# A hybrid encoder block in one kernel: the first receptance projection is taken from the unscaled input

## The chip, the cores and the metric

The kernel runs as one program on one core of a Trainium2 chip. The metric is the device time of one execution in microseconds (us); less is better. The engines of the core are named as the profile names them: PE is TensorE (PEld its weight load), DVE is VectorE, ACT is ScalarE, POOL is GpSimd, SP is SyncE, which issues most DMAs.

## The reference

One layer with 512 tokens of width 1024: an RMS norm, one wide input projection, three mixers (a gated convolution, an RG-LRU, and RWKV-7 time mixing), a gated merge, an output projection, and a squared-ReLU MLP. Cut to what the change touches:

```python
h = rms_norm(x, norm1_g[l])                 # x * rsqrt(mean(x^2) + eps) * g
p = h @ w_in[l]
pa, pb, pg, pc = _split(p, (COLS_A, COLS_B, COLS_GATE, COLS_C))
...
pc = token_shift(pc, rwkv_mu[l])            # p + (prev - p) * mu
r, k, v, xw, xa, xg = _split(pc, (D_C, D_C, D_C, R_W, R_A, R_G))
w_log = -jax.nn.softplus(-(rwkv_w0[l] + jnp.tanh(xw) @ rwkv_w2[l])) - 0.5
decay = jnp.exp(-jnp.exp(w_log))
a = jax.nn.sigmoid(rwkv_a0[l] + xa @ rwkv_a2[l])
g_c = jax.nn.sigmoid(xg) @ rwkv_g2[l]
kk = k * rwkv_kk[l]                         # then normalised by head
k = k * (1.0 + (a - 1.0) * rwkv_ka[l])
...
yc = rwkv7_recurrence(r, decay, k, v, kk, a)
```

The factor of the norm belongs to a token, and the projection sums over channels. So a projection may be taken from `x * g`, and its result multiplied by the factor of each token afterwards.

## The kernel before

**Layout.** All activations lie transposed: channels on the 128 partitions, the 512 tokens in the free dimension, so that a 128 x 512 tile is one eighth of the width and fills one PSUM tile. Every matmul of full precision is made of three (`mm3`, lines 152 to 155): each operand is split into a high and a low part, and high x high, high x low and low x high are summed. A projection of 128 output columns is thus 8 k tiles x 3 = 24 matmuls of 128 x 512 into one PSUM tile.

**Weights.** `load_w` (lines 123 to 137) fetches a weight tile in two halves. Each half is one DMA of SP into `raw` (3 buffers), a cast on ACT to `whi` (4 buffers) and a subtraction on DVE to `wlo` (4 buffers). These three get a higher priority, so that they stand in the queues well ahead of the matmuls that read them.

**PSUM.** Projections write to the pool `pp` of 3 tiles. Small products use `pm` (2 tiles), the recurrence `pc`.

**The prologue** (lines 204 to 336). `xT` is loaded. For each k tile ACT and DVE make `xgh` and `xgl`, the split of `x * g` without the token factor, and POOL, ACT, DVE and PE sum the squares into `pst`; `rsqrt_rows` turns these into `rsb`, the token factor on all partitions. Meanwhile PE projects from `xgh`, `xgl`: first `t_lr0` and `t_lr1`, the low-rank inputs (xw, xa and xg), and then `t_k0`, the first 128 columns of k (`proj_raw`, lines 258 to 260). Each of these PSUM tiles is multiplied by `rsb` as it is read, by DVE, into an SBUF tile `us0` or `us1` (`unscaled`, lines 296 to 299), from which `shift` (lines 282 to 284: one ACT and one DVE instruction) makes the token shift. `pro_scale` (lines 248 to 256) scales `xT` by `rsb` (five k tiles on POOL, three on DVE) and splits it into `hh` and `hl`, from which all later projections are taken (`proj`, lines 268 to 276).

**After the prologue.** Heads are worked on in four groups. `krv(g)` (lines 372 to 446) prepares k, r, v, decay and gates of a group: the norm of kk (`pn`), the decay (`pw`, then a scan), the gate (`pa`), and from them the tiles `AR` and `BK`. `amat` forms the products `pA` of these, masks them into `AXt` and transposes them to `Z`; `inverse` solves a triangular system on DVE in 31 dependent steps (`dg`, `Z`); `chain` runs the recurrence, `post` norms its result. `ab(q)` computes the two other mixers for 128 channels; it has eight projections (xb, gb, gatb, c, x, b, ga and, elsewhere, gc) and much elementwise work.

**What sets the order.** These parts are generators. `weave` runs a critical one (`krv(0)` first) step by step at a higher priority and, for each of its steps, a number of steps of a filling one (`AB[0]`, with the ratio `R0` = 0.852). A projection has four steps. Each instruction has a priority from where it was written and from the offsets; a scheduler then sets the order of every engine ahead of time, by its own estimate of when operands and buffers are ready. On the chip each engine takes its instructions strictly in this order, and waits in place for semaphores. A name with another number in an order (`pp_271`, `pp_430`) is another tile of the pool, not another buffer.

Of the kernel before, what the change touches and what calls it, by code (L numbers as in the profile page):

```python
# [9 lines left out]
F32 = mybir.dt.float32  # L10
# [8 lines left out]
P = 128  # L19
# [10 lines left out]
S = 512  # L30
# [54 lines left out]
COLS, CN = chunk_plan()  # L85
# [3 lines left out]
def block_kernel(ctx, tc, xt, win, par, mulr, sw, wout, w1, w2, fg, cst, eyes, out):  # L89
# [30 lines left out]
    pv = lambda n, j: part[:, PI[n], j:j + 1]  # L120


    def load_w(src):
        with tc.high_priority(offset=OFF):
            return load_w_(src)
# [10 lines left out]
    def load_w_(src):  # L136
        return [load_half(src, i) for i in range(2)]

    def wslice(w, kt):
        hi, lo = w[kt // 4]  # L140
        sl = slice((kt % 4) * P, (kt % 4 + 1) * P)
        return hi[:, sl], lo[:, sl]
# [49 lines left out]
    pp = ps.enter_context(tc.tile_pool(name="pp", bufs=3, space=PSUM))  # L192
# [65 lines left out]
    def proj_raw(w, t):  # L258
        for kt in range(KT):
            mm3(t, *wslice(w, kt), xgh(kt), xgl[:, kt], start=kt == 0, stop=kt == KT - 1)  # L260
# [7 lines left out]
    def proj(name):  # L268
        w = load_w(win[CN[name]])
        t = pp.tile([P, S], F32, tag="pp", name="pp")  # L270
        for kt in range(KT):
            wh, wl = wslice(w, kt)
            mm3(t, wh, wl, hh[:, kt], hl[:, kt], start=kt == 0, stop=kt == KT - 1)
            if kt % 2 == 1 and kt < KT - 1:
                yield
        return t
# [5 lines left out]
    def shift(pt, mu, omu, o):  # L282
        ac.activation(o, pt, AF.Copy, scale=omu)
        stt(o[:, 1:], pt[:, 0:S - 1], mu, o[:, 1:], MUL, ADD)
# [7 lines left out]
    def WP(tag, bufs=1):  # L292
        return pk.tile([P, S], F32, tag=tag, name=tag, bufs=bufs)


    def unscaled(t, tag):
        o = pro.tile([P, S], F32, tag=tag, name=tag)
        tt(o, t, rsb, MUL)
        return o
# [13 lines left out]
    OMK, OMR, OKA, OMV, N4, P4 = range(6)  # L313
    dvp = lambda i, j: dv[:, i, j:j + 1]
# [2 lines left out]
    shift(unscaled(t_lr0, "us0"), mul[:, 0:1], omul[:, 0:1], lr)  # L317
    t_k0 = pp.tile([P, S], F32, tag="pp", name="pp")
    proj_raw(load_w(win[CN[("k", 0)]]), t_k0)
    ac.activation(lr[0:64], lr[0:64], AF.Tanh)  # L320
    lws = sp.tile([P, S], F32R, name="lws")
    las = sp.tile([P, S], F32R, name="las")
# [10 lines left out]
    lgh, lgl = split(sp, lg, "lg")  # L333
    k0 = WP("ks")
    shift(unscaled(t_k0, "us0"), pv("mu_k", 0), dvp(OMK, 0), k0)
    pro_ctx.close()


# [27 lines left out]
    def c3(t):  # L366
        return t.rearrange("p (c t) -> p c t", c=NC)
# [4 lines left out]
    def krv(g, G_):  # L372
        G_.AR = pk.tile([P, 2, NC, 2, L], F32, tag="AR", name="AR")
        G_.BK = pk.tile([P, 2, NC, 2, L], F32, tag="BK", name="BK")
        G_.pl = sp.tile([P, 2, NC], F32, tag="pl", name="pl", bufs=2)
        G_.v = [sp.tile([P, S], F32, tag=f"v{h}", name=f"v{h}", bufs=2) for h in range(2)]
        G_.bv = [sp.tile([P, S], F32, tag=f"bv{h}", name=f"bv{h}", bufs=2) for h in range(2)]
        for jj in range(2):
            j = 2 * g + jj
            rs = WP("rs")  # L380
            if j == 0:
                ks = k0
            else:
                ks = WP("ks")
                t = yield from proj(("k", j))
                shift(t, pv("mu_k", j), dvp(OMK, j), ks)
            sq = WP("a1")
            ac.activation(sq, ks, AF.Square, scale=pv("kk", j))
            sqh, sql = split(pk, sq, "b")
            pn = pm.tile([P, S], F32, tag="pm", name="pn")  # L390
            pe.matmul(pn, bd, sqh, start=True, stop=False)
            pe.matmul(pn, bd, sql, start=False, stop=True)
            kk = WP("a5")
            rsqrt_rows(pk, kk, pn, 1e-24)
            stt(kk, ks, pv("kk", j), kk, MUL, MUL)
            yield
            t = yield from proj(("r", j))
            shift(t, pv("mu_r", j), dvp(OMR, j), rs)
            yield
            swh, swl = load_sw(pk, "swa", j, 0, 2)  # L400
            pw = pm.tile([P, S], F32, tag="pm", name="pw")
            pe.matmul(pw, swh[:, 0], lws, start=True, stop=False)
            pe.matmul(pw, swl[:, 0], lws, start=False, stop=True)
            sig = WP("a1")
            ac.activation(sig, pw, AF.Tanh, bias=pv("w0", j), scale=0.5)
            v.tensor_scalar(out=sig, in0=sig, scalar1=1.0, scalar2=None, op0=ADD)
            pa = pm.tile([P, S], F32, tag="pm", name="pa")
            pe.matmul(pa, swh[:, 1], las, start=True, stop=False)
            pe.matmul(pa, swl[:, 1], las, start=False, stop=True)
            av = WP("a4")  # L410
            ac.activation(av, pa, AF.Tanh, bias=pv("a0", j), scale=0.5)
            cum = WP("a2")
            v.tensor_tensor_scan(out=cum, data0=smk, data1=sig, initial=0.0, op0=MUL, op1=ADD)
            PP = pk.tile([P, NC, L + 1], F32, tag="PPt", name="PPt")
            gp.memset(PP[:, :, 0:1], 1.0)
            Pt = PP[:, :, 1:L + 1]
            ac.activation(Pt, c3(cum), AF.Exp, scale=-0.5 * CW)
            v.tensor_copy(G_.pl[:, jj], PP[:, :, L])
            pinv = WP("a3")
            ac.activation(pinv, cum, AF.Exp, scale=0.5 * CW)  # L420
            stt(G_.AR[:, jj, :, 0], c3(kk), -1.0, PP[:, :, 0:L], MUL, MUL)
            tt(G_.AR[:, jj, :, 1], c3(rs), Pt, MUL)
            t_ = WP("a1")
            stt(t_, av, 1.0, kk, ADD, MUL)
            stt(G_.BK[:, jj, :, 0], c3(t_), 0.5, c3(pinv), MUL, MUL)
            kp = WP("a2")
            ts2(kp, av, pv("ka", j), dvp(OKA, j), MUL, ADD)
            tt(kp, kp, ks, MUL)
            tt(G_.BK[:, jj, :, 1], c3(kp), c3(pinv), MUL)

            if jj == 0:
                rk = [WP(f"rk{h}") for h in range(2)]
            for h in range(2):
                r = slice(64 * h, 64 * h + 64)
                stt(rk[h][64 * jj:64 * jj + 64], rs[r], part[r, PI["rk"], j:j + 1], kp[r], MUL, MUL)
        rk = [split(pk, rk[h], ("a1", "a3") if h else "b") for h in range(2)]
        for h in range(2):
            q = 2 * g + h
            t = yield from proj(("v", q))
            shift(t, pv("mu_v", q), dvp(OMV, q), G_.v[h])  # L440
            yield
        for h in range(2):
            pb = pm.tile([P, S], F32, tag="pm", name="pb")
            for i in range(2):
                pe.matmul(pb, bd, rk[h][i], start=i == 0, stop=i == 1)
            tt(G_.bv[h], pb, G_.v[h], MUL)
# [450 lines left out]
    with tc.tile_pool(name="mw", bufs=2) as mw, \  # L897
# [12 lines left out]
        for fi in range(NF):  # L910
            t = pp.tile([P, S], F32, tag="pp", name="p1")
# [8 lines left out]
            r = mw.tile([P, S], F32, tag="r", name="r")  # L920
# [141 lines left out]
```

## Time and profile before

| | us |
|---|---|
| time, median of 3 runs | 1146.29 |
| lowest and highest of them | 1145.93 and 1151.92 |
| the profiled execution | 1150.27 |
| its span, from the first to the last record | 1148.5 |
| PE busy in the span | 1114.5 (97%) |
| DVE busy in the span | 787.4 (69%) |
| ACT busy in the span | 548.7 (48%) |
| mean granted clock of PE | 0.988 of full speed |

All times in the rows further down are in us from the start of the span. Busy times of PE are modelled from the starts of pipelined matmuls; a 128 x 512 matmul is shown with some 0.4 us, and the next one starts 0.23 us after it at full clock. A DVE row of 128 x 512 is shown with about 0.69 us, and the next starts 0.60 us after it, since the end of one overlaps the start of the next.

### The profile page before, as it was taken

How to read it: one execution, taken by the hardware profiler on the slowest of the kernel's cores; microseconds unless marked ns; L12 is line 12 of the kernel's file. 1: busy time of each engine (PE TensorE's matmuls, PEld its weight loads, DVE VectorE, ACT ScalarE, POOL GpSimd, SP SyncE). 2: the span in 40 equal slices, each digit the busy share in tenths (PEclk: the TensorE clock that was granted, in tenths of full speed). 3: DMA queues.
4: the chain of work that ended last, by engine and by line, in shares of the span. 5: the costliest groups of instructions: out<-in, count | busy, mean ns of one | idle time of the engine just before them, and what ended most of it. 6: DMA issues, size and time to landing. Idle time of an engine off the chain costs nothing.

```text
span 1148.5 us, 17262 instructions
## 1 busy us (share of the span) xinstructions
PE 1114.5 (97%) x6396; PEld 873.9 (76%) x6396; DVE 787.4 (69%) x1537; ACT 548.7 (48%) x1005; POOL 59.3 (5%) x99
## 2 busy tenths in 40 slices
PE   8899989999999999999999989999999999999996
PEld 4677876778777778777677767898888888888885
DVE  7998995879976889986889957686444444222225
ACT  6555455534556534557534465565444443222224
POOL 4100000000000000000000020100000000000003
PEclk9899998999999999999999999999999999999999
DMA  5221221222332122232222262455322225332232
GB/s 189 84 92 56 92 81 64 70 92 67 101 111 70 64 89 70 88 112 89 65 85 67 83 186 90 161 179 168 97 95 92 92 93 181 96 106 94 91 101 93
DMA packets 61973, 114.69 MB, mean 100 GB/s; under 512 B 7232, under 2 KB 10816, under 8 KB 61888
## 3 DMA queue, kind: packets, MB, share of 16 engines
q1 hardware_dynamic: 54960, 95.49, 26.2%
q0 software_dynamic: 6352, 17.30, 4.7%
q8 instruction: 50, 0.82, 0.3%
q10 hardware_dynamic: 576, 0.79, 0.2%
q14 instruction: 35, 0.29, 0.1%
HBM read 104.64 MB, written 8.91 MB: 99 GB/s over the span
## 4 chain that ended last, share of the span: by engine, by line
PE 81%; DVE 13%; issue 3%; DMA 1%; ACT 1%; POOL 0%; SPq 0%; DVEq 0%; ACTq 0%; POOLq 0%
PE pp L155 12%; PE pp L154 11%; PE pp L153 11%; PE acc L154 6%; PE acc L153 6%; PE acc L155 6%; PE p L153 5%; PE p L155 5%; PE p L154 5%; DVE wlo L94 3%; PE pA L458 2%; DVE Z L94 2%; DVE dg L94 2%; DVE g L97 1%; PE py L564 1%
## 5 line engine op out<-in xcount | busy, mean ns | idle before, releaser
L94 DVE TENSOR_TENSOR wlo<-raw,whi 128x512 fp32r<-128x512 f32 x340 | 235.4, 695 | 242.4 <-ACT whi L131 235.5
L131 ACT CAST whi<-raw 128x512 fp32r<-128x512 f32 x340 | 209.8, 619 | 364.2 <-PE acc L155 121.6
L155 PE MATMUL pp<-hh,wlo 128*128 128x512 f32 x696 | 285.8, 411 | 14.7 <-DVE wlo L94 14.5
L154 PE MATMUL pp<-hl,whi 128*128 128x512 f32 x696 | 282.3, 406 | 3.1 <-DVE hl L97 3.1
L153 PE MATMUL pp<-hh,whi 128*128 128x512 f32 x696 | 282.0, 407 | 1.3 <-ACT hh L254 1.3
L155 PEld LDWEIGHTS pp<-hh,wlo 128*128 128x128 f32 x696 | 132.6, 191 | 53.0 <-DVE wlo L94 21.6
L154 PEld LDWEIGHTS pp<-hl,whi 128*128 128x128 f32 x696 | 132.8, 191 | 34.8 <-DVE hl L97 3.7
L153 PEld LDWEIGHTS pp<-hh,whi 128*128 128x128 f32 x696 | 132.6, 191 | 32.8 <-ACT hh L254 1.8
L153 PE MATMUL p<-h2h,whi 128*128 128x512 f32 (+1 forms) x264 | 103.0, 390 | 0.0
L155 PE MATMUL p<-h2h,wlo 128*128 128x512 f32 (+1 forms) x264 | 102.9, 390 | 0.0
L154 PE MATMUL p<-h2l,whi 128*128 128x512 f32 (+1 forms) x264 | 102.8, 389 | 0.0
L154 PE MATMUL acc<-wlo,ah 128*128 128x512 f32 x256 | 99.7, 389 | 0.0
L155 PE MATMUL acc<-whi,al 128*128 128x512 f32 x256 | 99.6, 389 | 0.0
L153 PE MATMUL acc<-whi,ah 128*128 128x512 f32 x256 | 99.6, 389 | 0.0
L155 PEld LDWEIGHTS p<-h2h,wlo 128*128 128x128 f32 x264 | 49.7, 188 | 11.4
L154 PEld LDWEIGHTS p<-h2l,whi 128*128 128x128 f32 x264 | 49.7, 188 | 11.3
L153 PEld LDWEIGHTS p<-h2h,whi 128*128 128x128 f32 x264 | 49.7, 188 | 11.2
L154 PEld LDWEIGHTS acc<-wlo,ah 128*128 128x128 f32 x256 | 48.1, 188 | 10.3 <-DVE wlo L94 0.3
L155 PEld LDWEIGHTS acc<-whi,al 128*128 128x128 f32 x256 | 48.1, 188 | 10.0
L153 PEld LDWEIGHTS acc<-whi,ah 128*128 128x128 f32 x256 | 48.1, 188 | 9.8
L94 DVE TENSOR_TENSOR dg<-Z 64x31 f32<-64x31 f32 (+15 forms) x124 | 42.2, 340 | 4.0
L94 DVE TENSOR_TENSOR Z<-Z,dg 64x31 f32<-64x31 f32 (+15 forms) x124 | 42.2, 340 | 4.0
(299 smaller groups left out, 1536.6 us busy)
## 6 DMA issues: line engine op xcount, KB each, us to landing
raw<-in_win SPq DMA_DIRECT2D x180, 256.0 KB, 2.6
raw<-in_w SPq DMA_DIRECT2D x128, 256.0 KB, 2.6
raw<-in_wout SPq DMA_DIRECT2D x32, 256.0 KB, 2.7
swr<-in_sw SPq DMA_DIRECT2D x16, 128.0 KB, 2.1
x2T<-in_xt POOLq DMA_DIRECT2D x4, 512.0 KB, 6.7
x2d<-st POOLq DMA_DIRECT2D x8, 256.0 KB, 2.9
xr<-x2d POOLq DMA_DIRECT2D x1, 2048.0 KB, 9.1
xT<-in_xt SPq DMA_DIRECT2D x3, 512.0 KB, 6.1
```

The costliest lines, as they stand in the source:

```text
L94: return v.tensor_tensor(out=o, in0=a, in1=b, op=op)
L97: return v.scalar_tensor_tensor(out=o, in0=a, scalar=s, in1=b, op0=op0, op1=op1)
L131: ac.copy(hi, raw)
L153: pe.matmul(ps, wh, xh, start=start, stop=False)
L154: pe.matmul(ps, wh, xl, start=False, stop=False)
L155: pe.matmul(ps, wl, xh, start=False, stop=stop)
L458: pe.matmul(pts[h][:, ci], G_.BK[rows, jj, c], G_.AR[rows, jj, c], start=True, stop=True)
L564: mm = pe.matmul(py[64 * h:64 * h + 64, jj], w, x, start=first and jj == 0, stop=last, skip_group_check=True)
```

## The change

A fourth raw projection is written behind `t_k0` in the prologue: `t_r0`, the first 128 columns of r, from `xgh` and `xgl`. At the prologue's end its PSUM tile is multiplied by `rsb` into `us1` and shifted into `r0`. In `krv` the first pass (j = 0) takes `r0` for `rs`, and skips the projection from `hh` and `hl`, its shift, and the four steps that these had. The matmuls are as many as before; added is one DVE product of 128 x 512.

```diff
--- before.py
+++ after.py
@@ -317,6 +317,8 @@
     shift(unscaled(t_lr0, "us0"), mul[:, 0:1], omul[:, 0:1], lr)
     t_k0 = pp.tile([P, S], F32, tag="pp", name="pp")
     proj_raw(load_w(win[CN[("k", 0)]]), t_k0)
+    t_r0 = pp.tile([P, S], F32, tag="pp", name="pp")
+    proj_raw(load_w(win[CN[("r", 0)]]), t_r0)
     ac.activation(lr[0:64], lr[0:64], AF.Tanh)
     lws = sp.tile([P, S], F32R, name="lws")
     las = sp.tile([P, S], F32R, name="las")
@@ -333,6 +335,8 @@
     lgh, lgl = split(sp, lg, "lg")
     k0 = WP("ks")
     shift(unscaled(t_k0, "us0"), pv("mu_k", 0), dvp(OMK, 0), k0)
+    r0 = WP("rs")
+    shift(unscaled(t_r0, "us1"), pv("mu_r", 0), dvp(OMR, 0), r0)
     pro_ctx.close()
 
 
@@ -377,11 +381,10 @@
         G_.bv = [sp.tile([P, S], F32, tag=f"bv{h}", name=f"bv{h}", bufs=2) for h in range(2)]
         for jj in range(2):
             j = 2 * g + jj
-            rs = WP("rs")
             if j == 0:
-                ks = k0
+                rs, ks = r0, k0
             else:
-                ks = WP("ks")
+                rs, ks = WP("rs"), WP("ks")
                 t = yield from proj(("k", j))
                 shift(t, pv("mu_k", j), dvp(OMK, j), ks)
             sq = WP("a1")
@@ -394,9 +397,10 @@
             rsqrt_rows(pk, kk, pn, 1e-24)
             stt(kk, ks, pv("kk", j), kk, MUL, MUL)
             yield
-            t = yield from proj(("r", j))
-            shift(t, pv("mu_r", j), dvp(OMR, j), rs)
-            yield
+            if j > 0:
+                t = yield from proj(("r", j))
+                shift(t, pv("mu_r", j), dvp(OMR, j), rs)
+                yield
             swh, swl = load_sw(pk, "swa", j, 0, 2)
             pw = pm.tile([P, S], F32, tag="pm", name="pw")
             pe.matmul(pw, swh[:, 0], lws, start=True, stop=False)
```

The scheduler makes a new order from this. The number of instructions on each engine is the same but for that product. Three places, with the waits that each instruction has (the number behind a semaphore's name tells nothing here):

PE, from the place where the raw projections of the prologue give way to the first one from `hh` and `hl`. Before (`pp_271` is k0 and `pp_430` is r0):

```order
L153 MATMUL pp_271<-xgh_91,whi_274 128x512
L153 MATMUL pp_430<-hh_73,whi_420 128x512 [waits Activation_49]
L154 MATMUL pp_271<-xgl_93,whi_274 128x512
L155 MATMUL pp_271<-xgh_91,wlo_276 128x512
L153 MATMUL pp_271<-xgh_91,whi_274 128x512
L154 MATMUL pp_430<-hl_74,whi_420 128x512 [waits DVE_49]
L155 MATMUL pp_430<-hh_73,wlo_422 128x512
L153 MATMUL pp_430<-hh_73,whi_420 128x512
L154 MATMUL pp_430<-hl_74,whi_420 128x512 [waits DVE_49]
```
With the change (`pp_308` is r0, now raw, and `pp_511` is k1, the second tile of k):

```order
L154 MATMUL pp_308<-xgl_93,whi_317 128x512
L155 MATMUL pp_308<-xgh_92,wlo_319 128x512
L153 MATMUL pp_308<-xgh_92,whi_317 128x512
L154 MATMUL pp_308<-xgl_93,whi_317 128x512
L153 MATMUL pp_511<-hh_73,whi_501 128x512 [waits DVE_49,Activation_49]
L154 MATMUL pp_511<-hl_74,whi_501 128x512
L155 MATMUL pp_511<-hh_73,wlo_503 128x512
L153 MATMUL pp_511<-hh_73,whi_501 128x512
L154 MATMUL pp_511<-hl_74,whi_501 128x512
```
Before, the two kinds were mixed from the eighth matmul of k0 on. Now all 24 of k0 and 23 of r0 stand ahead of the first `hh` matmul, which is the 103rd matmul row on PE (row 102; the first of k0 is row 55 in both orders), and which has a wait on DVE of its own. The five behind it have none, nor have the `hl` ones up to the sixth k tile. The 24th of r0 stands behind all of k1.

DVE, the end of the scaling of the input, with the reading of the second low-rank tile (`pp_232` is lr1). Before:

```order
L94 TENSOR_TENSOR wlo_442<-raw_438,whi_440 128x512 [waits DMAHW6_49,PE_49,Activation_49]
L97 SCALAR_TENSOR_TENSOR hl_74<-xT_90,n1t_99,hh_73 128x512 [waits Pool_49]
L97 SCALAR_TENSOR_TENSOR hl_74<-xT_90,n1t_99,hh_73 128x512 [waits Activation_49]
L94 TENSOR_TENSOR lws_309<-ks_266,lws_309 64x512
L94 TENSOR_TENSOR wlo_448<-raw_444,whi_446 128x512 [waits DMAHW7_49,PE_49,Activation_49]
L94 TENSOR_TENSOR las_310<-ks_266,las_310 64x512
L94 TENSOR_TENSOR us1_341<-pp_232,rsb_94 128x512
L97 SCALAR_TENSOR_TENSOR hl_74<-xT_90,n1t_99,hh_73 128x512 [waits Pool_49]
```
With the change:

```order
L97 SCALAR_TENSOR_TENSOR hl_74<-xT_90,n1t_99,hh_73 128x512 [waits Activation_49]
L94 TENSOR_TENSOR wlo_509<-raw_505,whi_507 128x512 [waits DMAHW7_49,PE_49,Activation_49]
L97 SCALAR_TENSOR_TENSOR hl_74<-xT_90,n1t_99,hh_73 128x512 [waits Activation_49]
L94 TENSOR_TENSOR lws_346<-ks_266,lws_346 64x512
L97 SCALAR_TENSOR_TENSOR hl_74<-xT_90,n1t_99,hh_73 128x512 [waits Pool_49]
L94 TENSOR_TENSOR wlo_523<-raw_519,whi_521 128x512 [waits DMAHW0_49,PE_49,Activation_49]
L94 TENSOR_TENSOR las_347<-ks_266,las_347 64x512
L94 TENSOR_TENSOR us1_378<-pp_232,rsb_94 128x512
L97 SCALAR_TENSOR_TENSOR hl_74<-xT_90,n1t_99,hh_73 128x512 [waits Pool_49] x2
```
The product `us1` from `pp_232` stood at row 58 and stands at row 59; the weight halves between the `hl` rows are of k1 and xb now, and were of xb.

DVE, after this, with the low parts of the next weights (`wlo_529` is the second half of xb, `wlo_616` and `wlo_622` are r1; before, `wlo_555` is k1). Before:

```order
L97 SCALAR_TENSOR_TENSOR hl_74<-xT_90,n1t_99,hh_73 128x512 [waits Pool_49]
L94 TENSOR_TENSOR us0_352<-pp_271,rsb_94 128x512
L100 TENSOR_SCALAR rs_340<-rs_340 128x512 [waits Activation_49]
L345 RECIPROCAL spt1_358<-spt1_358 128x8
L94 TENSOR_TENSOR wlo_555<-raw_551,whi_553 128x512 [waits DMAHW1_49,PE_49,Activation_49]
L94 TENSOR_TENSOR lgl_348<-rs_340,lgh_347 128x512 [waits Activation_49]
L97 SCALAR_TENSOR_TENSOR ks_351<-us0_352,part_66,ks_351 128x511 [waits Activation_49]
L94 TENSOR_TENSOR spt0_357<-spt0_357,spt1_358 128x8 [waits DVE_49]
L97 SCALAR_TENSOR_TENSOR rs_391<-pp_430,part_66,rs_391 128x511 [waits Activation_49]
```
With the change:

```order
L100 TENSOR_SCALAR rs_377<-rs_377 128x512 [waits Activation_49]
L94 TENSOR_TENSOR wlo_529<-raw_525,whi_527 128x512 [waits DMAHW1_49,PE_49]
L94 TENSOR_TENSOR spt0_399<-spt0_399,spt1_400 128x8 [waits DVE_49]
L94 TENSOR_TENSOR spt1_400<-spt0_399 128x8 [waits DVE_49]
L94 TENSOR_TENSOR lgl_385<-rs_377,lgh_384 128x512 [waits Activation_49]
L97 SCALAR_TENSOR_TENSOR ks_388<-us0_389,part_66,ks_388 128x511 [waits Activation_49]
L352 TENSOR_SCALAR spt2_401<-spt1_400 128x8 [waits DVE_49]
L97 SCALAR_TENSOR_TENSOR spt2_401<-spt2_401,spt1_400 128x8 [waits DVE_49] x2
L94 TENSOR_TENSOR wlo_616<-raw_612,whi_614 128x512 [waits DMAHW2_49,PE_49]
L94 TENSOR_TENSOR us1_394<-pp_308,rsb_94 128x512 [waits PE_49]
L94 TENSOR_TENSOR wlo_622<-raw_618,whi_620 128x512 [waits DMAHW3_49,Activation_49]
```
The low parts of two projections move ahead of the norm of k; the reading of `t_r0` (`us1` from `pp_308`) stands between them, and the shift from PSUM of r0 (`rs` from `pp_430`) is gone from here.

Further on, the first matmul `pA` of `amat` is row 321 of PE before and row 282 with the change, as fewer steps of `ab` are woven into `krv(0)`. The first transpose to `Z` on DVE is row 186 before and row 181 with the change. From row 393 of PE, row 220 of DVE and row 121 of ACT on, the two orders have the same instructions in the same places to the end.

## Rows read from the trace of the kernel before

**Rows 1.** The page, busy time of TensorE, its share and its instructions.

```profile
PE 1114.5 (97%) x6396; PEld 873.9 (76%) x6396; DVE 787.4 (69%) x1537; ACT 548.7 (48%) x1005; POOL 59.3 (5%) x99
```

**Rows 2.** Stretches of 20 us: PE, PEld, DVE, ACT, POOL busy, PE clock, DMA.

```profile
20.00:40.00 20.00, 15.58 (x55) 11.83 (x54) 18.26 (x36) 11.91 (x19) 8.02 (x5) 0.83 0.25 78
...
60.00:80.00 20.00, 19.79 (x85) 15.65 (x84) 19.58 (x50) 11.86 (x21) 0.11 (x1) 1.00 0.29 89
```

**Rows 3.** Waits, 24 to 46 us: who waited for whom, total, times, longest.

```profile
PE pp L154 <- DVE hl L97: 3.1, 1, 3.1
...
PE pp L153 <- ACT hh L254: 1.3, 1, 1.3
```

**Rows 4.** Timeline of TensorE, 25 to 50 us: start, duration, [idle before, releaser].

```profile
25.02 0.40 PE L153 MATMUL pp<-xgh,whi 128*128 128x512 f32 x1
...
26.41 0.40 PE L153 MATMUL pp<-xgh,whi 128*128 128x512 f32 x1
...
32.42 0.79 PE L154 MATMUL pp<-hl,whi 128*128 128x512 f32 x1 [3.07 <-DVE hl L97]
...
38.13 0.46 PE L155 MATMUL pp<-xgh,wlo 128*128 128x512 f32 x1
...
42.63 0.40 PE L153 MATMUL pp<-hh,whi 128*128 128x512 f32 x1
...
49.89 0.39 PE L154 MATMUL pp<-hl,whi 128*128 128x512 f32 x1
```

**Rows 5.** Stretches around the gaps, columns as in rows 2.

```profile
29.36:32.42 3.06, 0.00 (x0) 0.00 (x0) 3.06 (x3) 1.44 (x3) 2.46 (x2) 0.84 0.22 52
32.42:38.20 5.78, 5.78 (x14) 4.52 (x15) 5.24 (x8) 3.48 (x6) 0.00 (x0) 0.50 0.12 36
...
161.20:164.50 3.30, 3.30 (x9) 2.55 (x9) 3.11 (x6) 3.00 (x6) 0.00 (x0) 0.50 0.50 157
```

**Rows 6.** Timeline of VectorE, 23 to 46 us.

```profile
23.69 0.69 DVE L94 TENSOR_TENSOR us<-pp,rsb 128x512 f32<-128x512 f32 x1
...
28.94 1.75 DVE L94 TENSOR_TENSOR wlo<-raw,whi 128x512 fp32r<-128x512 f32 x1
...
32.95 0.68 DVE L94 TENSOR_TENSOR xT<-xT,rsb 128x512 f32<-128x512 f32 x1
33.55 0.74 DVE L97 SCALAR_TENSOR_TENSOR hl<-xT,n1t,hh 128x512 fp32r<-128x512 f32 x1
34.22 0.68 DVE L94 TENSOR_TENSOR xT<-xT,rsb 128x512 f32<-128x512 f32 x1
```

**Rows 7.** Timeline of ScalarE, 23 to 46 us.

```profile
33.67 0.72 ACT L254 ACTIVATE hh<-xT,n1t 128x512 fp32r<-128x512 f32 x1 [2.86 <-DVE xT L94]
```

**Rows 8.** The tiles `us`, who writes and reads them: ns, least, median, most.

```profile
L94 DVE TENSOR_TENSOR us<-pp,rsb x3: 684/691/691, 23.7 to 45.2; 128x512 f32<-128x512 f32 x3
...
L97 DVE SCALAR_TENSOR_TENSOR rs<-us,mul,rs x1: 751/751/751, 43.9 to 43.9; 128x511 f32<-128x511 f32 x1
```

**Rows 9.** Groups of VectorE by form, 23 to 110 us: busy us, mean ns.

```profile
L97 DVE SCALAR_TENSOR_TENSOR rs<-pp,part,rs 128x511 f32<-128x511 f32 x2 | 1.5, 746 | 0.1
```

**Rows 10.** Timeline of VectorE, 46 to 112 us.

```profile
51.79 0.72 DVE L174 STREAM_TRANSPOSE rqw<-pn 128x512 f32<-128x512 f32 x1
...
85.16 0.69 DVE L97 SCALAR_TENSOR_TENSOR BK<-a,a 128x512 f32<-128x512 f32 x1
...
106.04 2.06 DVE L482 STREAM_TRANSPOSE Z<-AXt 32x1024 f32<-32x1024 f32 x1
```

**Rows 11.** Two more stretches, columns as in rows 2.

```profile
32.95:43.60 10.65, 10.65 (x37) 8.38 (x36) 8.48 (x14) 5.53 (x9) 0.50 (x1) 0.75 0.17 51
...
60.00:70.00 10.00, 9.79 (x42) 7.61 (x41) 9.96 (x22) 5.70 (x10) 0.11 (x1) 1.00 0.26 81
```

**Rows 12.** Timeline of TensorE, 95 to 135 us.

```profile
95.81 1.16 PE L458 MATMUL pA<-AR,BK 64*128 64x128 f32 x8
```

**Rows 13.** Timeline of TensorE, 140 to 172 us.

```profile
160.23 0.50 PE L155 MATMUL pp<-hh,wlo 128*128 128x512 f32 x1 [3.24 <-DVE wlo L94]
```

## The prediction, made before the changed kernel was run

> **What bounds the kernel now.** I read the page first: TensorE is busy 1114.5 us, 97% of the span [rows 1]. So a change can only be worth what TensorE loses by idling or by running at half clock near the place that is touched. The stretches of 20 us come next [rows 2]: TensorE has only 15.58 us of work in 20 to 40, at a mean clock of 0.83, and 19.79 in 60 to 80; VectorE is at 18.26 and 19.58 of 20 in the same two. The list of waits names the two gaps: 3.1 us for `hl` of VectorE and 1.3 us for `hh` of ScalarE [rows 3]. The TensorE timeline places them [rows 4]: the raw projection of k0 (operands `xgh`, `xgl`) is mixed with the first one of the scaled input (`hh`, `hl`), and the engine, which takes matmuls in order, stands at 26.8 and at 29.4 behind an `hh` or `hl` matmul while later raw ones could run. The clock fell to its lower level (0.50, 1.2 GHz) during the second gap and stayed there until 38.2 [rows 5].
>
> What this place costs today: from the first k0 matmul (25.02) to the first matmul of the next tile but one (42.63) lie 43 matmuls [rows 4]. At a pitch of 0.2335 us (six starts from 25.02 to 26.41 give 0.232, 31 from 42.63 to 49.89 give 0.234) that is 10.04 us of 17.61. **Lost: 7.57 us**, 0.66% of the time. That is the most the change can save here.
>
> **The change, part by part.**
>
> *The 24 raw matmuls of r0 follow k0 without a gap.* Their weights take the places on ScalarE and VectorE that the same weights had before; the last of the four, a low part, is done at 30.69 [rows 6], ahead of its reader at 33.9. Their PSUM tile is the one of lr0, read by the `us` at 23.69. So 24 of k0 and 23 of r0 run from 25.02 to 25.02 + 47 x 0.2335 = 36.0. Both old gaps are filled.
>
> *The next matmul then waits for PSUM.* The pool `pp` has three tiles and four projections now want one. r0 took that of lr0; k1, next in the order, takes that of lr1, which is free when the `us` of lr1 has read it. On VectorE this is behind the scaling and splitting of the input. Up to the `xT` at 32.95 the rows are those of before. From there eleven rows stand ahead of the `us`: xT twice, wlo three times, lws and las at 0.605 (32.95 to 33.55 is 0.60), and hl four times at 0.67 (33.55 to 34.22) [rows 6], which is 4.24 + 2.68 = 6.92. The `us` runs from 39.87 to 40.56; TensorE goes on at about 40.65. No ScalarE operand is later: `hh` of the third k tile is cast at 33.67 [rows 7], and the second weight cast behind it ends near 35.6, before VectorE asks at 36.1. **New gap: 36.1 to 40.65, 4.55 us**, in place of 1.35 + 3.06.
>
> *The clock.* After 4.4 us of gaps 13 starts took 5.71 us (32.42 to 38.13) instead of 3.04: 2.7 lost. After the one gap of 3.24 that ended at 160.23 the half-clock stretch was 161.2 to 164.5; 3.3 us at 0.427 a matmul instead of 0.2335 lose 1.5 [rows 4, 5, 13]. The new gap is as long as the first two together and unbroken like the last: I take 2.0, between these ends, 1.5 and 2.7. The 24 matmuls of k1 then end at 40.65 + 24 x 0.2335 + 2.0 = 48.25, with 71 matmuls since 25.02 (16.58 us). Lost: 23.23 - 16.58 = 6.65. **-0.9 us** against 7.57.
>
> *The extra VectorE product.* `us` costs 0.69, of which 0.60 is ahead of the next row as in all such products [rows 6, 8]. The shift then reads SBUF where it read PSUM: 0.751 for the shift from `us`, 0.746 for the two from `pp` [rows 8, 9], so nothing. The Trainium skill ("Perfetto Trace Analysis", Optimizing Scalar/DVE Operations) gives VectorE about 125 ns of overhead on PSUM and 60 on SBUF, and ScalarE the reverse; by that the shift would gain some 0.07 us on VectorE, and the rows do not bear it out. **+0.6 us on VectorE.**
>
> *VectorE now waits once for TensorE.* After the `us` it runs `hl` twice, a shift, a `us` and a small one to 43.6. Its next row, the low part of the second xb weight, needs a weight buffer that is free after the first half of k1, eleven matmuls from 40.65 at 0.427: 45.4, done 45.9. A wait of 2.3 (at full clock none). Queued behind it are the splits and the k0 shift. These run 0.6, 0.3, 0.6 and 0.7 to 48.25; the square, one weight cast and the cast `bh` on ScalarE 3 x 0.62 to 50.2; TensorE, seven matmuls beyond 48.25, would be at `pn` at 49.9. So `pn` is 0.4 late, and VectorE transposes it at 51.85, against 51.79 before [rows 10]. The cover of that wait is that VectorE was idle 10.65 - 8.48 = 2.17 us of 32.95 to 43.60 before [rows 11] and now isn't.
>
> *The first key/value stage has less to hide behind.* Its generator has four steps fewer, so 3.4 fewer steps of the gate branch are woven in, and the first `pA` matmul stands 39 rows earlier on TensorE (row 282 for 321). What TensorE meets: the tile of xb (24 matmuls) must be copied by ScalarE, behind the r1 copy that waits for `rk` on VectorE near 60.8; the copy ends at 62.7, TensorE arrives at 61.5, +1.2. The k1 tile is read by its shift at 65.7, +0.4. With `pn` that is +2.0, against 0.2 idle in 60 to 70 before [rows 11]. TensorE reaches row 282 at 87.05; before it was there 39 x 0.2335 ahead of 95.81 [rows 12], at 86.7. **TensorE +0.3.** VectorE writes the last `BK` at 84.9 (85.16 before [rows 10]). The mask products follow at once, and the transposes `Z` begin at 103.5 for 106.04 [rows 10]; but between them and the 220th row, from which the two orders of VectorE are the same, lie now 4 wide products, a scan and a split (4 x 0.72 + 1.24 + 0.28 = 4.4) that stood ahead of `Z` before. The step `dg` begins 3.8 earlier (there was a scan ahead of it) and ends 0.6 late. **VectorE +0.6.**
>
> *The end.* From TensorE's row 393 and VectorE's row 220 on both orders are row for row the same to the last. The stage ends in a gap of 3.24 us where TensorE waits for `wlo` behind the transposes of VectorE (157.0 to 160.23 [rows 13]). So VectorE's +0.6 decides and TensorE's +0.3 vanishes in that gap. Sum for the profiled execution: 1150.27 + 0.6. That execution lies 4.0 above the median of 1146.29, with the same instructions; the difference is applied to the median: 1146.9, **1147.0**.
>
> **Rivals.**
>
> *It fills the gap for good.* TensorE never stands between 25 and 46, the clock stays up: -7.57 + 0.6, so 1139.3. For it: the raw matmuls need nothing that is late. Against it: the PSUM tile of lr1. `us` would have to come 4 us earlier on an engine that is full until 35 [rows 2, 6]. The Trainium skill ("Perfetto Trace Analysis", Matmuls) wants independent groups in rotation over PSUM banks so that reading one overlaps the next; by that rule a fourth raw tile on three banks stalls, and the order of the change bears it out. 0.05.
>
> *The clock does not fall.* One gap of 4.55, but 11 us of unbroken matmuls ahead of it. The 2.0 go, the VectorE wait at 43.6 with them: -2.2 + 0.6 - 0.2, so 1144.5. Against it: it fell in or within 1 us after both gaps of over 3 us [rows 5, 13]. 0.13.
>
> *Slower: VectorE waits for the one r0 matmul that was left behind.* The last of r0's 24 stands behind all 24 of k1. If the four `wlo` buffers were handed out in turn, the weight product that stands at 43.6 would need the buffer this matmul reads, free at 48.7, not 45.9. Then VectorE loses 2.8 more, `pn` comes at 53.0, TensorE stands 3 us ahead of it and may fall to half clock again (1.5), and the next weights come late in turn, 2.9 more on VectorE by the same working (low part of the first gb weight at 61.9 for 57.0). VectorE would be 0.6 + 2.8 + 2.9 = 6.3 late at its 220th row: 1152.6. For it: VectorE has nothing to spare there. Against it: the third weight product on (the first of r1) has a wait on TensorE of its own, and the one behind it none; handed out in turn it would be needless. It decides from a wait of over 4 us. 0.12.
>
> **How the numbers follow.** Forecast 0.70 (1145 to 1150, the clock's 1.5 to 2.7 and a further step of 1.5 at one of the short gaps, and executions that differ by 4 as those shown do); the others 0.05, 0.13, 0.12. Range 1143.0 to 1152.0: it leaves out the first rival and two thirds of the last, some 0.14 with the tails. About 0.5% (5.7 us) is what a measurement of this kernel can tell from no change: faster is under 1140.6, slower over 1152.0. Faster 0.06, same 0.83, slower 0.11.
>
> **What would show it.** Right: no gap of TensorE before 36; one of about 4.5 us before the first `hh` matmul, ended by `us` of VectorE, then half clock; VectorE idle near 44 for TensorE; `pn` near 51, first `pA` near 87, `Z` near 103.5, and the gap near 157 to 160 still there. Wrong: `us` of lr1 ending before 37, gaps of over 2 us between 48 and 90, or `Z`'s last step ending more than 3 us from where it did.

## The result, and the profile after

| | before | with the change |
|---|---|---|
| time, median of 18 runs each | 1151.27 us | 1154.45 us |
| lowest and highest | 1145.30, 1155.70 | 1149.51, 1156.31 |
| the profiled execution | 1150.27 | 1154.50 |
| its span | 1148.5 | 1152.7 |

The ratio is 1.0028, with a 95% interval of 1.0015 to 1.0040: the change costs some 3.2 us (1.7 to 4.6). That is within the 0.5% that was called no change, but clear of zero, and the time of 1154.45 lies above the forecast range, which ended at 1152.0.

The page, busy time, answers [rows 1]: each engine has the instructions of before, and VectorE one product more.

```profile
PE 1116.8 (97%) x6396; PEld 874.8 (76%) x6396; DVE 787.8 (68%) x1538; ACT 549.1 (48%) x1005; POOL 59.4 (5%) x99
```

TensorE's waits after the change, over the whole span (who waited for whom: total, times, longest). In place of the two of [rows 3] stand one for `us`, and one for ScalarE's copy of xb (line 656):

```profile
PE pp L155 <- DVE wlo L94: 15.0, 10, 3.7
PE pp L153 <- DVE us L94: 5.1, 1, 5.1
...
PE pp L153 <- ACT u L656: 1.0, 1, 1.0
```

TensorE's timeline after the change, with the gaps of [rows 4, 13], the first `pA` of [rows 12], and the gate products `pga`, `pgi` with the last `pA` behind them:

```profile
36.61 0.39 PE L154 MATMUL pp<-xgl,whi 128*128 128x512 f32 x1
42.08 0.77 PE L153 MATMUL pp<-hh,whi 128*128 128x512 f32 x1 [5.08 <-DVE us L94]
...
63.66 0.50 PE L153 MATMUL pp<-hh,whi 128*128 128x512 f32 x1 [0.96 <-ACT u L656]
...
88.30 0.93 PE L462 MATMUL pA<-AR,BK 64*128 64x128 f32 x6
...
101.38 0.39 PE L153 MATMUL pga<-uh,swbh 128*128 128x512 f32 x1
...
102.51 0.39 PE L155 MATMUL pgi<-uh,swbl 128*128 128x512 f32 x1
103.14 2.04 PE L462 MATMUL pA<-AR,BK 64*128 64x128 f32 x16
...
163.05 0.80 PE L155 MATMUL pp<-hh,wlo 128*128 128x512 f32 x1 [3.69 <-DVE wlo L94]
```

VectorE's timeline after the change; `us`, `rqw`, `BK` and `Z` answer [rows 6, 10], and `rsb`, the first step `dg` and its first transpose are the marks by which the experiments are compared:

```profile
23.85 0.71 DVE L181 STREAM_TRANSPOSE rsb<-rqq 128x512 f32<-128x512 f32 x1
...
41.24 0.69 DVE L94 TENSOR_TENSOR us<-pp,rsb 128x512 f32<-128x512 f32 x1
...
46.92 0.69 DVE L94 TENSOR_TENSOR wlo<-raw,whi 128x512 fp32r<-128x512 f32 x1 [1.88 <-PE pp L155]
...
52.82 0.72 DVE L174 STREAM_TRANSPOSE rqw<-pn 128x512 f32<-128x512 f32 x1
...
85.79 0.69 DVE L97 SCALAR_TENSOR_TENSOR BK<-a,a 128x512 f32<-128x512 f32 x1
...
89.70 0.69 DVE L94 TENSOR_TENSOR bv<-pb,v 128x512 f32<-128x512 f32 x1 [0.35 <-PE pb L449]
...
91.67 0.69 DVE L94 TENSOR_TENSOR wlo<-raw,whi 128x512 fp32r<-128x512 f32 x1 [0.67 <-ACT whi L131]
...
96.46 0.69 DVE L94 TENSOR_TENSOR AXt<-pA,mask 128x512 f32<-128x512 f32 x1 [0.76 <-PE pA L462]
99.23 0.69 DVE L94 TENSOR_TENSOR wlo<-raw,whi 128x512 fp32r<-128x512 f32 x1 [2.08 <-ACT whi L131]
102.04 0.69 DVE L94 TENSOR_TENSOR wlo<-raw,whi 128x512 fp32r<-128x512 f32 x1 [2.12 <-ACT whi L131]
103.41 0.43 DVE L94 TENSOR_TENSOR swbl<-swr,swbh 128x256 fp32r<-128x256 f32 x1 [0.67 <-ACT swbh L366]
...
104.61 1.30 DVE L94 TENSOR_TENSOR AXt<-pA,mask 128x512 f32<-128x512 f32 x2
105.94 4.16 DVE L486 STREAM_TRANSPOSE Z<-AXt 32x1024 f32<-32x1024 f32 x2
...
110.85 0.19 DVE L94 TENSOR_TENSOR dg<-Z 64x31 f32<-64x31 f32 x1
...
161.20 1.23 DVE L508 STREAM_TRANSPOSE dg<-Z 32x1024 f32<-32x1024 f32 x1
```

The last three marks before the change, VectorE's timeline of the first profile ([rows 10] has its `Z`):

```profile
22.95 0.71 DVE L181 STREAM_TRANSPOSE rsb<-rqq 128x512 f32<-128x512 f32 x1
...
112.23 0.19 DVE L94 TENSOR_TENSOR dg<-Z 64x31 f32<-64x31 f32 x1
...
158.38 1.23 DVE L504 STREAM_TRANSPOSE dg<-Z 32x1024 f32<-32x1024 f32 x1
```

To be read here: the profile of after starts 0.90 late (`rsb`). From `rsb` to the first transpose of `dg` it takes 137.35 for 135.43, **1.9 us more**. The first step `dg` is earlier (87.0 us after `rsb` for 89.3), and from it to the transpose take 50.35 for 46.15, **4.2 more**: the wide rows that moved behind `Z`. So `dg` had to come 4.2 earlier to break even, and came 2.3 earlier (`Z` 1.0; a scan that stood between the two is gone from there).

A table by stretch shows the rest. Stretches of the profile after (columns as in [rows 2]; the sixth figure behind the busy times is the granted clock): the gap ahead of k1, the half clock behind it, and the half clock around the last gap, whose answer before is in [rows 5].

```profile
37.00:42.08 5.08, 0.00 (x0) 0.03 (x1) 4.99 (x9) 2.14 (x5) 0.00 (x0) 0.71 0.30 83
42.08:46.00 3.92, 3.92 (x9) 3.11 (x10) 2.96 (x6) 1.75 (x3) 0.00 (x0) 0.50 0.12 44
...
162.03:168.86 6.83, 5.81 (x14) 4.55 (x15) 6.17 (x10) 6.00 (x10) 0.00 (x0) 0.50 0.27 79
```

Behind the gap at 163 TensorE ran 5.81 us at the lower level, for 3.3 before. From the transpose of `dg` to the first `pG` (171.00, before 167.11) take 9.80 for 8.73: **1.07 more**. 1.92 + 1.07 = 3.0 us, and with the start of 0.9 and 0.35 later on, that is the 4.2 between the two spans.

### The profile page after: what moved, and what is told of

Its sections match the earlier page's. It is cut to its first block, busy times and chain, and to the rows that moved or that the text cites. A ratio compares the mean times of both kernels' runs of the same rounds, so it can differ in the third digit from the quotient of the medians.

```text
span 1152.7 us, 17264 instructions
## 1 busy us (share of the span) xinstructions
PE 1116.8 (97%) x6396; PEld 874.8 (76%) x6396; DVE 787.8 (68%) x1538; ACT 549.1 (48%) x1005; POOL 59.4 (5%) x99
## 4 chain that ended last, share of the span: by engine, by line
PE 79%; DVE 16%; issue 3%; ACT 2%; DMA 1%; SPq 0%; ACTq 0%; DVEq 0%
PE pp L155 11%; PE pp L153 11%; PE pp L154 10%; PE acc L154 6%; PE acc L153 6%; PE acc L155 6%; PE p L153 5%; PE p L155 5%; PE p L154 5%; DVE wlo L94 3%; PE pA L462 2%; DVE Z L94 2%; DVE dg L94 2%; DVE g L97 2%; PE py L568 1%
## 5 line engine op out<-in xcount | busy, mean ns | idle before, releaser
L154 PE MATMUL pp<-hl,whi 128*128 128x512 f32 x688 | 279.5, 406 | 0.0
```

Of the source, the lines that this page charges most:

```text
L154: pe.matmul(ps, wh, xl, start=False, stop=False)
```

## The experiments

Each is read by the same marks of one profiled execution. The last `BK`, `Z`, the first `dg` and its transpose are given in us after `rsb`; the times are ratios to the kernel before, with 95% intervals, where a kernel was timed.

| kernel | last BK | Z | dg | transpose of dg | time ratio |
|---|---|---|---|---|---|
| before | 62.2 | 83.1 | 89.3 | 135.4 | 1 |
| before again (e7) | 62.4 | 83.2 | 89.4 | 135.6 | |
| change | 61.9 | 82.1 | 87.0 | 137.4 | 1.0028 [1.0015, 1.0040] |
| change again (e6) | 61.7 | 81.8 | 86.7 | 137.1 | |
| e1 order of before behind | 60.8 | 82.1 | 88.3 | 134.4 | 1.0009 [0.9988, 1.0030] |
| e2 idle PSUM tile | 60.2 | 81.6 | 86.5 | 136.8 | 1.0029 [1.0007, 1.0051] |
| e3 both | 59.6 | 81.9 | 88.1 | 134.2 | 1.0004 [0.9978, 1.0030] |
| e4 before, less fill | 60.4 | 80.2 | 85.1 | 135.4 | 1.0002 [0.9980, 1.0023] |
| e5 both, lr1 read early | 57.9 | 80.1 | 86.3 | 132.4 | 0.9965 [0.9942, 0.9987] |
| e8 as e5, no idle tile | 60.4 | 81.6 | 87.8 | 133.9 | |
| e9 as e5, less fill | 60.2 | 80.3 | 85.2 | 135.5 | |
| e10 before, lr1 read early | 60.2 | 81.5 | 87.7 | 133.8 | |
| e11 change, gate products later | 62.0 | 75.9 | 80.9 | 132.4 | 1.0035 [1.0021, 1.0049] |
| e12 e9, gate products later | 59.3 | 73.1 | 78.1 | 129.6 | 1.0026 [1.0009, 1.0042] |

**e6 and e7: each kernel once more.**

> The changed kernel once more, for a second profiled execution. If what the change costs is in its order, the same gaps stand in the trace (about 5.1 us ahead of the first hh matmul, 1.0 near 64, 3.7 near 163), and from the reading of rsb, the token factor, to the first transpose of dg it takes 137.3 us again, give or take 0.5. If the start before 24 us (rsb at 23.85 for 22.95) and the length of the half clock behind the gap at 163 (6.8 us for 3.4) belong to the change, they are the same here too; if they are of the execution, they differ.

> The kernel before once more. From rsb to the first transpose of dg 135.4 us again, give or take 0.5, and a first gap of 1.35 and a second of 3.07 us. If the start is of the execution and not of the kernel, rsb lies somewhere between 22.5 and 26.5, and the half-clock stretches behind 160 us differ from those of the first profile.

The stretch repeats: 137.05 and 137.35, 135.55 and 135.43. So do the gaps (5.06, 0.96, 3.69), and the 1.07 behind the last gap (9.79 and 9.80; before 8.72 and 8.73). The starts don't: `rsb` at 24.17 and 26.14. So 1.5 to 1.9 + 1.07 belong to the change, 2.6 to 3.0 us, and that agrees with the timed runs (1.7 to 4.6). The start is of the execution.

**e1: the order of before behind the raw r0.** The edit, in the first pass of `krv`:

```diff
+            else:
+                for _ in range(4):
+                    yield
```

> The kernel with the change, but the first pass of the key/value stage keeps four empty steps in place of the skipped projection of r, so that as many steps of the gate branch are woven in as before the change. r0 is still raw. The scheduler then puts the first pA matmul at TensorE's row 321 (282 with the change, 321 before it) and the two Z transposes at VectorE's rows 186 and 188, as before; the wait of k1 for the PSUM tile of lr1 stays. Theory O (the loss sits in the order behind the prologue: with fewer fill steps the last pA products stand behind a whole projection and the gate products, so Z is not earlier while five wide VectorE rows have moved behind it): about as long as before, -0.5 us, from -1.0 to +0.6, ratio 0.999 to 1.0005; the step dg begins near 112 and ends within 1 us of where it did. Theory G (the loss is the gap ahead of k1 and the half clock behind it): as long as with the change, +3 us, ratio 1.002 to 1.004, with a gap of about 5 us near 36 to 42.

The stretch is 134.4, 2.8 under the change and 1.1 under before. The prologue is the same, gap and all; TensorE's timeline of e1:

```profile
42.26 0.76 PE L153 MATMUL pp<-hh,whi 128*128 128x512 f32 x1 [4.83 <-DVE us L94]
...
95.84 1.16 PE L465 MATMUL pA<-AR,BK 64*128 64x128 f32 x8
...
160.27 0.50 PE L155 MATMUL pp<-hh,wlo 128*128 128x512 f32 x1 [3.22 <-DVE wlo L94]
```

So the gap is not what costs: with it, the raw r0 is worth 1.1 us (the forecast said 0.9 for TensorE). What costs is the order behind. The 1.07 us behind the last gap are gone too (167.15 - 158.42 = 8.73 from the transpose of `dg` to `pG`, as before). The time, 1.0009, has too wide an interval to tell 0 from 2.8 us by itself.

**e2 and e3: r0 in the idle PSUM tile**, without and with the four empty steps:

```diff
-    t_r0 = pp.tile([P, S], F32, tag="pp", name="pp")
+    t_r0 = pc.tile([P, S], F32, tag="pS", name="pS")
```

> The kernel with the change, but r0 is written to a PSUM tile that stands idle in the prologue (that of pS) instead of the third tile of the projections' pool; so k1 can take the tile of lr0 and does not wait for the reading of lr1. The scheduler also mixes k1 into r0 again (first hh matmul at TensorE's row 70, for 102 with the change and 62 before). The later order has fewer fill steps, as with the change (first pA at row 272, last at 335). Theory G: the gap of 5.1 and the 1.8 us lost at half clock go, TensorE is 6 to 7 us ahead at 48, and the time is 3 to 4 us under before, ratio 0.9965. Theory O: TensorE's lead ends where it waits for VectorE in the key/value stage; VectorE is as full as before and has the same five wide rows behind Z, so 0 to +2.5 us, ratio 1.000 to 1.002, and gaps of TensorE between 48 and 90 of 3 us or more in sum.

> Both at once: r0 in the idle PSUM tile and the four empty steps. All 24 matmuls of k0 and 24 of r0 stand ahead of the first hh matmul (row 103), and the order behind is that of before (pA from row 321 on, Z at VectorE's rows 186 and 188). Theory O: no gap in the prologue, and no row moved behind Z; TensorE leads by 7 us at 48 and keeps what VectorE's one extra row and its own waits for VectorE leave, -2 to -6 us, ratio 0.995 to 0.998. Theory G: the same sign, -6 to -7 us, ratio 0.994 to 0.995. If VectorE alone sets the end of this stage, whatever its order, the gap near 160 grows by all of the lead and the time is +0.6, ratio 1.0005.

e2 fell on theory O's side: the gap is gone from its place, but the scheduler mixed k1 into r0, and two others (1.60 and 1.67) and a half-clock stretch came back; behind them ScalarE's copy of xb is waited for (1.59, where theory O named 3 or more), and the stretch is 136.8. As the prologue's order changed too, e2 is not e3 without fill steps alone. e3 is a miss of the expectation: the gap is there, since xb now takes lr1's tile, one row behind the first of k1.

```profile
41.26 0.51 PE L153 MATMUL pp<-hh,whi 128*128 128x512 f32 x1 [4.60 <-DVE us L94]
```

That is TensorE's timeline of e3. A fourth tile moves the wait to the next projection, as long as lr1 is read at VectorE's 60th row.

**e4: the kernel before with fewer fill steps, and nothing else.**

```diff
-    weave(krv(0, GS[0]), AB[0], R0)
+    weave(krv(0, GS[0]), AB[0], R0 * 17 / 21)
```

> The kernel before, with nothing raw added: only the ratio of the first weave is lowered from 0.852 to 0.852 x 17/21 = 0.690, so that as many steps of the gate branch are woven into the first key/value stage as with the change (14.5 for 17.9). The scheduler puts pA at TensorE's rows 292 to 339 and Z at VectorE's rows 180 and 181 (with the change 282 to 336, and 181 and 182; before 321 to 344, and 186 and 188). Theory O: this alone costs what the change costs, +2 to +3.5 us, ratio 1.002 to 1.003, with Z no more than 1 us earlier and dg ending 2 to 3 us late. Theory G: nothing, -0.5 to +0.5 us, ratio 0.9995 to 1.0005.

A miss for theory O as it was put, and what theory G said: the sparser weave alone costs nothing (135.4, ratio 1.0002). VectorE's timeline of e4:

```profile
82.85 0.69 DVE L97 SCALAR_TENSOR_TENSOR BK<-a,a 128x512 f32<-128x512 f32 x1
...
102.67 4.16 DVE L482 STREAM_TRANSPOSE Z<-AXt 32x1024 f32<-32x1024 f32 x2
...
107.58 0.19 DVE L94 TENSOR_TENSOR dg<-Z 64x31 f32<-64x31 f32 x1
```

It too has 4.2 more from `dg` on (50.32), but `dg` comes 4.2 earlier after `rsb`, which the change did not get. TensorE's timeline tells why: the last `pA` products before the change, and below them the first and the last ones of e4.

```profile
103.53 1.16 PE L458 MATMUL pA<-AR,BK 64*128 64x128 f32 x8
```

```profile
88.76 1.54 PE L458 MATMUL pA<-AR,BK 64*128 64x128 f32 x16
...
99.87 2.04 PE L458 MATMUL pA<-AR,BK 64*128 64x128 f32 x16
```

`Z` follows the last group of `pA` on TensorE at a steady distance: 2.5 us in the seven profiles with the order of before (106.04 - 103.53), 2.8 in the five with fewer fill steps (105.94 - 103.14 with the change, 102.67 - 99.87 in e4). From 70 us to that group the profiles show no wait of TensorE of over 0.2 us, while VectorE does wait: with the change 2.08, 2.12 and 0.67 us ahead of its last two mask products, each time for a cast of ScalarE. So TensorE's place in its order sets `Z`, not the work of VectorE. In the order of before, `Z` stands 10.2 us behind the first `pA` in all six kernels that have it (106.04 - 95.81, e1 106.08 - 95.84, e3, e5, e8 and e10 alike), and what TensorE gains is handed on. With fewer fill steps the first `pA` comes much earlier, but more 128 x 512 matmuls then stand between the first and the last: 5 before, 26 in e4, 36 with the change. Counted from `rsb`, the change has the first `pA` 8.4 us earlier than before and the last only 1.3 (79.3 for 80.6); e4 has the last 3.2 earlier (77.4). So the sparser order makes up for its rows behind `Z` in e4, and not with the change.

**e5, e9, e8, e10: lr1 read early.** e5 is e3 with

```diff
     with tc.high_priority(offset=OFFS):
+        u_lr1 = unscaled(t_lr1, "us1")
         pro_scale()
     lg = WP("rs")
-    shift(unscaled(t_lr1, "us1"), mul[:, 1:2], omul[:, 1:2], lg)
+    shift(u_lr1, mul[:, 1:2], omul[:, 1:2], lg)
```

e9 leaves the four empty steps out of it, e8 the idle tile, and e10 has this edit alone in the kernel before.

> The kernel with the change, with three edits at once: r0 in the idle PSUM tile of pS, the four empty steps in place of the skipped projection, and the reading of lr1's PSUM tile (us1) written ahead of the scaling of the input, at that priority, so that VectorE reads it at its row 45 (60 without). Then neither k1 nor xb has to wait for a PSUM tile behind 36 us; the first hh matmul stands at TensorE's row 103, and the order behind is that of before (pA from row 321, Z at VectorE's rows 186 and 188). Theory T (TensorE's place in its own order decides when the last pA products come, and with the order of before each us that it gains there is a us at the last step of dg, until the last BK of VectorE, some 10 us ahead of the first pA, becomes the bound): no gap of over 1 us from 25 to 45, clock up, 6 to 7 us less lost than before in 20 to 50, first pA near 90 to 91, Z near 101, and the time -4 to -6.5 us, ratio 0.9945 to 0.9965. Theory V (VectorE, full from 25 to 88 us, sets the end of the stage): pA or the last matmuls ahead of the gap near 160 wait for it, the last step of dg is +0.6 where it was, and the time -0.5 to +0.6, ratio 0.9995 to 1.0005.

> As e5 but without the four empty steps: r0 in the idle tile and the early reading of lr1, with fewer fill steps behind (first pA at TensorE's row 280, last at 339, Z at VectorE's rows 180 and 181). If the order with fewer fill steps costs what it cost with the change against e1, 2.7 us from rsb to the first transpose of dg whatever stands ahead of it, this is 132.4 + 2.7 = 135.1, within 0.7, with a wait of TensorE of about 1 us or more between 55 and 70 and the last pA products behind the gate products again. If fewer fill steps only cost where TensorE comes late out of the prologue, 132.0 to 133.0.

> As e5 but r0 stays in the projections' pool: early reading of lr1 and the four empty steps, without the idle PUM tile of pS. Measured by the stretch from rsb to the first transpose of dg, which repeated within 0.3 us in the runs so far (before 135.4 and 135.6, with the change 137.4 and 137.1, e1 134.4, e5 132.4). Now k1 takes the tile of lr1, free early, and xb (TensorE's row 118) that of k0, which VectorE reads near 43.5, as in e1 and e3: TensorE runs to row 117 with some 2 us of short waits for the scaled input and stands there for 2 to 3 us. If TensorE's place sets Z, the stretch is between e1 and e5: 133.0 to 134.0. If the idle tile is not needed, 132.4 as e5; if the early reading alone is nothing, 134.4 as e1.

> The kernel before with nothing but the early reading of lr1's tile (VectorE's row 46 for 58); r0 is projected from the scaled input as before. If the early reading helps only where a raw projection follows that would wait for that tile, TensorE's two gaps (1.35 and 3.07) stay within 0.7 and the stretch from rsb to the first transpose of dg is 135.0 to 136.2, for 135.4 and 135.6. If it is a gain of its own, 133 to 134.

e5 is the one kernel here that is faster than before: 0.9965, some 4.0 us (1.5 to 6.7). TensorE's timeline of e5, and below it two stretches of 20 us:

```profile
38.29 0.50 PE L153 MATMUL pp<-hh,whi 128*128 128x512 f32 x1 [1.75 <-ACT whi L131]
39.81 0.50 PE L155 MATMUL pp<-hh,wlo 128*128 128x512 f32 x1 [0.79 <-DVE wlo L94]
...
48.82 0.50 PE L395 MATMUL pn<-bh,bd 128*128 128x512 f32 x1 [1.26 <-ACT bh L148]
```

```profile
20.00:40.00 20.00, 17.46 (x75) 13.52 (x74) 19.59 (x42) 13.96 (x23) 9.30 (x7) 1.00 0.31 102
40.00:60.00 20.00, 18.59 (x78) 14.09 (x78) 19.68 (x54) 11.24 (x20) 0.00 (x0) 1.00 0.31 92
```

No wait for PSUM of over 0.2 us is left, the clock stays at its upper level in these 40 us, and VectorE is now busy 19.6 of each 20 us (before, 18.26 in the first [rows 2]). The time is at the lower end of theory T. The first `pA` is at 92.8 for 90 to 91, and of the 7.6 us lost before, 3.0 arrive at the transpose of `dg`: TensorE now waits for casts and low parts of the weights, and for `pn`. e9 came as expected in number: without the empty steps 135.5, 3.1 more (`dg` 1.1 earlier, and 4.2 of rows behind it). But its prologue is not that of e5: k1 is mixed into r0 as in e2, with two gaps (1.60 and 1.67) and a half-clock stretch, so the 3.1 can't be put down to the fill steps alone. The pairs that differ in these only are before and e4, and e1 and the change. e8 shows that the idle tile is needed too (133.9, and a gap of 4.25 ahead of xb where 2 to 3 was expected; VectorE's reading of k0's tile and a cast of ScalarE end within 0.1 us of each other there, and the profile names the cast). e10 fell on the second of its two alternatives: the early reading is a gain of its own, 1.7 us. The second gap is 2.40 for 3.07, and the half clock behind it was 3.4 us long for 6.8. Which of the moved rows does that was not tried.

**e11 and e12: the gate products behind the last `pA`.** In `ab`, ahead of `load_sw`:

```diff
+        if q == 6:
+            yield
```

> The changed kernel with one empty step ahead of the gate products pga and pgi of the first block of the gate branch, and nothing else. The scheduler then puts all of the pA products ahead of them: the last stands at TensorE's row 312 for 336, and with it the projection c and the gate products fall behind Z's transposes (VectorE's rows 177 and 179). The prologue is that of the change, with its gap of 5 us. Theory N (what makes the change slower is that its last two pA tiles stand behind the projection c and the gate products, so that Z comes no earlier though VectorE's wide rows were moved behind it): last pA near 97 for 104.9, from rsb to the first Z 74 to 77 us for 82.0, and from rsb to the first transpose of dg 131.5 to 135 for 137.4 and 137.1, since some more wide rows now lie behind Z; time -1 to -4 us against before, ratio 0.9965 to 0.999. If the loss is in the prologue or wherever fewer fill steps are woven in, 136.5 to 137.5 and a ratio of 1.002 to 1.004.

> The same empty step in e9: r0 in the idle tile of pS, the early reading of lr1, fewer fill steps, and all pA products ahead of the gate products (TensorE's rows 280 to 313). By theory N from rsb to the first transpose of dg as much less than e9's 135.5 as e11 is less than 137.2: 130 to 133, and the time under before by 3 to 6 us, ratio 0.9945 to 0.9975, about that of e5 or better. If e9's loss against e5 lies elsewhere, 135 to 136 and a ratio near 1.

The place of the loss is shown: with this one empty step 11 wide matmuls stand between the first and the last `pA`, not 36, `Z` comes 6.2 us earlier, and the stretch is 132.4, 4.8 under the change's. But the time did not follow, against the expectation of both (1.0035 and 1.0026). TensorE's waits of e11, and its clock behind the new one:

```profile
PE pp L153 <- DVE us L94: 5.1, 1, 5.1
PE pT L521 <- ACT dg L515: 2.7, 1, 2.7
```

```profile
181.08:191.32 10.24, 10.24 (x78) 7.03 (x74) 2.51 (x7) 4.45 (x12) 0.00 (x0) 0.50 0.16 49
```

The gate block is now late in its turn: where TensorE comes to `pT` at 179.84, it waits 2.72 us for ScalarE's copy of `dg` (e12: 4.03), which before it met without a wait, and the clock is at half for 10.2 us from there (e12: 13.7), for 6.8 with the change. The 4.8 us were given back one stage later: from `rsb` to the first transpose of the second group's `dg` e11 takes 299.85, the change 299.30 and 298.95. The mark of `dg` thus stands for the time only where the stage behind it runs as before; in e11 and e12 it does not.

## Why the prediction was wrong, point by point

- **What bounds, and the prologue: right.** TensorE ran without a gap to 37.0. Then came one gap of 5.08 for `us` (4.55 foreseen; four of VectorE's handoffs ahead of it were some 0.1 longer than was taken). At half clock it lost 3.92 x (1 - 0.2335 / 0.427) = 1.8 (2.0 foreseen). VectorE's wait at 46.92 was 1.88 (2.3), `pn` was transposed at 51.9 when the late start of 0.9 is taken off (51.85), and the wait for xb's copy was 0.96 (1.2). e1 gives the sum: -1.1 for -0.9.
- **The key/value stage: right up to `BK`.** With 0.9 of late start taken off, the first `pA` is at 87.4 (87.05 foreseen), the last `BK` at 84.9 (84.9).
- **"The mask products follow at once, and the transposes `Z` begin at 103.5": the step that failed.** They began at 105.0 by the same count, 17.6 after the first `pA`, for 16.45. The last two mask products did not follow at once: they waited for the last two `pA` tiles, which TensorE reached 14.84 us after the first (103.14 - 88.30), and `Z` came 2.80 behind these. VectorE's own small waits were not it: those of 0.35 and 0.67 end in one for TensorE (0.76 at 96.46). So even with the first `pA` at the foreseen 87.05, these two distances put `Z` at 104.7. The other half of the step, 4.4 us of rows behind `Z`, measured 4.2. So VectorE was 1.5 to 1.9 late, not 0.6: a small difference of two large terms, one of them sized too low. The prediction gives no working for its 16.45 us and does not name what stands between the sixth and the seventh `pA` tile: a projection and the gate products, which use the two `pm` tiles as `pA` does; e11, which puts them behind, shows that they are worth 6.2 us of `Z`.
- **"TensorE's +0.3 vanishes in that gap": incomplete.** The gap near 160 did take TensorE's lateness. But behind it the clock stayed low for 5.8 us instead of 3.3, in both executions of the change: +1.07. It was not foreseen. In the rows the low stretch began inside the gap with the change (at 162.03, the gap ended at 163.05), and behind it before (161.2 for 160.23) and in e9 (161.6 for 160.40), which has a gap of the same 3.69 and had 3.4 us of half clock. Why a stretch that begins earlier is longer is not explained.
- **The base: the larger part of the miss in the number.** The difference was put on the median of the three runs shown, 1146.29. The median of 18 is 1151.27. That is 5.0 of the 7.5 us by which the forecast of 1147.0 was low; the rest, some 2.5, is the size of the change, 3.2 for 0.6. On 1151.27 the same forecast would have been 1151.9, and its range, moved along, 1148.0 to 1157.0, with 1154.45 in it; the 0.6 would still lie outside the measured 1.7 to 4.6. The profiled execution (1150.27), which was read as lying high, was near the median.
- **The rivals.** The first (filled for good) was rightly given little: it took an early reading, a fourth tile and the old order together (e5), and then brought 4.0, not 7.0. The clock did fall. The straggler of r0 did not bite: VectorE's wait at 46.92 was 1.88, not 4 or more. The range's upper end allowed for VectorE's mishaps only from that straggler.
- The Trainium skill ("Perfetto Trace Analysis", Matmuls) asks for independent groups in rotation over PSUM banks, so that the reading of one overlaps the next. e3 and e5 bear it out with a condition: a fourth tile alone left a gap of 4.60, and only with the early reading did the wait for PSUM go.

## What to carry to other kernels

A schedule that is laid out ahead changes far from the edit: see in the new order what now stands between the first and the last of the products on which the next stage waits, and price that, not only the place of the edit. When the forecast is a difference of two moves of about 4 us, its range must be as wide as the error of either. A gain at an early stage is worth something only if the next stage is bound by the engine that gained, and moving a loss out of one stage can bring it back in the next (e11).

## What the runs showed that was not expected

Two executions of one kernel differ most where nothing was changed. Stretches of the two profiles of the kernel before, first the first one, then e7 (columns as in [rows 2]):

```profile
0.00:25.00 25.00, 20.97 (x60) 12.32 (x61) 19.05 (x44) 15.77 (x27) 7.94 (x16) 1.00 0.62 206
...
480.00:510.00 30.00, 26.73 (x111) 20.38 (x110) 24.66 (x41) 15.38 (x27) 1.08 (x2) 1.00 0.39 118
```

```profile
0.00:25.00 25.00, 20.13 (x47) 11.04 (x48) 16.37 (x37) 13.68 (x24) 7.12 (x15) 1.00 0.59 196
...
480.00:510.00 30.00, 26.68 (x98) 19.90 (x97) 24.48 (x41) 12.87 (x22) 1.62 (x3) 0.89 0.38 114
```

In e7 `rsb` is 3.2 us late, with fewer instructions done in the first 25 us, though the clock is up in both; from there to the transpose of `dg` the two agree to 0.1; and behind a gap that both have (2.69 us to 493.10, 2.68 to 496.50 in e7) the clock fell in e7 (mean 0.89) and not in the first (1.00). The spans differ by 7.2 us. The stretch between two marks inside one execution repeated within 0.3 us, so one profile of each kernel told larger differences than that apart; by the time, 12 runs gave intervals of 3 to 6 us.
